# A ScalarE copy moved ahead of its slot's work, and the products of sixteen tokens moved to slots of their own, in a hybrid decoder layer with product-key experts

## The chip, the cores and the metric

The kernel runs on one core of one Trainium2 chip. A core has five engines that run their own instruction streams: TensorE (PE, with its weight loads as PEld), VectorE (DVE), ScalarE (ACT), GpSimd (POOL) and SyncE (SP), which here only issues DMAs. They meet through semaphores. The metric is the device time of one execution in microseconds; the median of three runs before the change is 1067.83 us (1067.64 to 1069.07).

## The reference

One decoder layer on 256 tokens of width 1024: attention of two kinds, gated and projected, then an expert layer. The change lies in the expert layer, of which this is the core:

```python
def peer_ffn(h, wq, subkeys, u, v):
    q = (hf @ wq).reshape(T, PEER_HEADS, 2, PEER_QDIM // 2)
    s = jnp.einsum('thpd,hpnd->thpn', q, subkeys).astype(jnp.float32)
    s1, i1 = lax.top_k(s[:, :, 0], PEER_TOPK)
    s2, i2 = lax.top_k(s[:, :, 1], PEER_TOPK)
    ...
    top_s, pos = lax.top_k(cand, PEER_TOPK)
    idx = jnp.take_along_axis(cand_idx, pos, axis=-1)
    w = jax.nn.softmax(top_s, axis=-1)
    ...
        act = jax.nn.gelu(jnp.einsum('cd,chkd->chk', x_c, u[idx_c]).astype(jnp.float32), approximate=False)
        coef = (w_c * act).astype(v.dtype)
        return jnp.einsum('chk,chkd->cd', coef, v[idx_c])
```

Each token chooses 16 of 128 x 128 experts in each of 8 heads, 128 choices in all. An expert is one row of u and one of v. Its number is a pair of keys below 128.

## The kernel before

**The dense form.** The kernel doesn't gather the experts' rows for most tokens. It multiplies all 16384 rows of u with the tokens, puts gelu on the result, multiplies it with each token's weight for that expert (zero for most), and then multiplies by all of v. Both matrices are read once, as 128 blocks of 128 experts. G[0] and G[1] hold the coefficients of blocks 0 to 63 and 64 to 127, each as 128 partitions x 64 blocks x 256 tokens in f32. The first 16 tokens (NG) go another way: their rows of u are gathered by indirect DMA, eight tokens at a time, the dot products are formed on VectorE, and their coefficients come to the blocks at the end. The other 240 tokens (TD) go through u in the dense form.

**Slots.** A slot (`slot`, L235) handles one block of weights. It issues the fetches of the blocks two and three ahead on SP's queue (L237, L238), then what is in `first`, then for the block two ahead the high part on ScalarE (L192, `whi`) and the low part on VectorE (L196, `wlo`), then what is in `late` (L250), then what is in `pre` (L251 to L253), and then the block's matmuls (L364: 24 of them, high part with the high and the low part of the tokens, low part with the high part). `raw`, `whi` and `wlo` have three buffers each. Each engine runs its instructions in the order in which they are issued here; only semaphores hold one back for another. So the order in a slot is written out by hand, and the place in the slot decides behind what an instruction stands on its engine.

**Two slots make a pair of u.** `u_pair` (L1211) puts the products of two blocks into one buffer `pj`, and one slot later, through `late`, `evac` brings them out with gelu: for the tokens whose weights are already in G to `gt` (L1227), then VectorE multiplies that into G (L1231); for the others to G itself (L1229). The first 32 pairs run while VectorE still chooses the experts. The change lies in the last 32 pairs, slots 0 to 63 of the second half of u. What runs in which of these slots is written out by `at_slot` (L1336 to L1355); jobs of one slot run in the order in which they were listed.

**The weights of the tokens come to the blocks as one-hot products.** For a group k of eight tokens (30 groups) VectorE makes one-hot rows of the first and the second keys (`hot_keys`, L1274) and multiplies the second with the weights, in f16 (`hot_high`, L1285). ScalarE makes the rest of the weight, four tokens in one slot and four in the next (`hot_low`, L1281). In slot 2k + 2 PE sums the 16 products (`hot_sum`, L1293) to a tile `pw` of two PSUM banks, of which there are two (`wide`, L1264). In slot 2k + 3 `hot_use` brings them to G: for the blocks whose gelu is there, VectorE multiplies into G (L1302, once for G[0] and once for G[1]); for the blocks that are still to come, ScalarE copies the product to G[1] (L1304), where gelu is multiplied on later. The one-hot tile has two buffers.

**The sixteen tokens.** `dot` (L1089) runs in every fourth slot, from 9 to 37, and asks for the next gather. `dots_end` and `coefs_in` bring the coefficients around through DRAM and one small transpose (L1118) in slots 39 and 42. Then, for each eight tokens, `few_keys` (L1312 twice, L1316 three times, VectorE), `few_sum` (L1322: 24 matmuls to a `pw` tile) and `few_use` (L1328, two copies on ScalarE to G[0] and G[1]). Their tables lie where the residual x2 lay; it was written to DRAM and comes back by four DMAs on POOL's queue (`x2_in`, L1073), which must wait for the last `few_sum`. The v stage after the last slot begins with transposes of x2 (L1406).

Of the kernel before, what the change touches and what calls it, by code (L numbers as in the profile page):

```python
# [14 lines left out]
AF = mybir.ActivationFunctionType  # L15
# [4 lines left out]
P = 128  # L20
# [10 lines left out]
TG = 8  # L31
PACE = 1.22
WARM = 15
WSCALE = 32768.0
# [103 lines left out]
def body(tc, nc, a):  # L138
# [137 lines left out]
    def table(f):  # L276
        nc.scalar.activation(junk, ones, f)
# [31 lines left out]
    def w1_load(j, hf):  # L309
        r = slice(8 * hf, 8 * hf + 8)  # L310
        nc.sync.dma_start(w1[:, j, r], a["w1"][:, j, r])
# [153 lines left out]
    def rope(name, dst, parts):  # L465
        raw = ropes[name]
        rp = bank("pS")
        nc.tensor.matmul(rp, K["rt"], flat(raw), start=True, stop=True)
        t = wk.tile([P, 2, T], F32, name="ropetmp", bufs=1)
        nc.vector.tensor_tensor(t, halves(rp), stab[:, None, :].to_broadcast([P, 2, T]), OP.mult)  # L470
        nc.vector.tensor_tensor(raw, raw, ctab[:, None, :].to_broadcast([P, 2, T]), OP.mult)
        dst = raw if dst is None else dst
        nc.vector.tensor_tensor(dst, raw, t, OP.add)
        halve(*parts, dst)
# [9 lines left out]
    def cmp_windows(j):  # L484
        win = wins[j] = wk.tile([P, 2, 8, 2, NCMP], F32, name="win")
        src = kcb[:, j].rearrange("p g (n l r) -> p g n l r", l=8, r=2)
        for hf in range(2):
            for g in range(2):
                nc.vector.tensor_tensor(
                    win[:, hf, :, g, :], src[:, g, hf:hf + NCMP, :, 0].rearrange("p n l -> p l n"),  # L490
                    pos[:, j, hf * 8:hf * 8 + 8, None].to_broadcast([P, 8, NCMP]), OP.add)

    def cmp_hidden(j):
        hp = bank("pS")
        for lp in range(16):
            nc.tensor.matmul(hp[:30, :P], flat(wins[j][:, lp // 8, lp % 8]), w1[:, j, lp], start=(lp == 0),  # L496
                             stop=(lp == 15))
        ht[j] = wk.tile([P, 30], F32, name="ht")
        hn = wk.tile([30, P], F32, name="hn")
        nc.scalar.activation(hn, hp[:30, :P], AF.Gelu)  # L500
        if j:
            table(AF.Exp)

        def back():
            tp = bank("pO")
            nc.tensor.transpose(tp[:, :30], hn, ident[:30, :30])
            nc.vector.tensor_copy(ht[j], tp[:, :30])
        backs.append(back)
# [208 lines left out]
    def y_turn(n, q2):  # L717
        tp = bank("pT")
        for j in range(2):
            cc = q2 * 2 + j  # L720
            for b in range(2):
                nc.tensor.transpose(tp[:, j * T + b * P:j * T + (b + 1) * P], y[:, b, n, cc * P:(cc + 1) * P], ident)
        c0 = n * 4 + q2 * 2
        hv = flat(bh[:, c0:c0 + 2])
        nc.scalar.activation(hv, tp, AF.Copy)
        nc.vector.tensor_tensor(flat(bl[:, c0:c0 + 2]), tp, hv.bitcast(F32), OP.subtract)
# [59 lines left out]
    def sv_evac(acc):  # L786
# [11 lines left out]
         pre=((fg_log, lambda: cmp_windows(0)), (lambda: table(AF.Gelu), fg_rest, lambda: rope("k", None, (krope[:, 0, 0], krope[:, 1, 0])), swap, lambda: cmp_windows(1), lambda: w1_load(1, 0))))  # L798
    pair(lambda pj: rope_in("q1", pj, 0.125), ah, al,
         pre=((lambda: cmp_hidden(0), fg_logs, lambda: w1_load(1, 1)), (cmp_back, lambda: cmp_hidden(1), lambda: rope("q0", nqt[:, 0:2], (nqs[:, 0, 0:2], nqs[:, 1, 0:2])))))  # L800
# [8 lines left out]
    for m in range(8):  # L809
        pre = [[tick], [tick]]  # L810
        if m == 5:
            pre = [[tick, lambda: y_turn(1, 0)], [tick, lambda: y_turn(1, 1)]]
        if m == 7:
            pre = [[], [lambda: y_turn(0, 0), lambda: y_turn(0, 1)]]
# [70 lines left out]
    G = [ga.tile([P, 64, T], F32, name="G0"), None]  # L885
# [173 lines left out]
    def tokens_out(q):  # L1059
        nc.gpsimd.dma_start(xhs[q].rearrange("(g t) d -> g t d", t=TG),  # L1060
                            xhd[None, q * TG:(q + 1) * TG, :].to_broadcast([P // TG, TG, D]))
# [5 lines left out]
    def x2_out(k):  # L1067
        sb, dr = x2_part(k)
        nc.gpsimd.dma_start(dr, sb)
# [5 lines left out]
    def tokens_in(q):  # L1075
        nc.gpsimd.dma_start(flat(x2[1]), xhs[q])
# [4 lines left out]
    def rows_in(n):  # L1081
        q, j = divmod(n, TG)
        nc.gpsimd.indirect_dma_start(rows_of_step(n), None, a["u_n"],
                                     bass.IndirectOffsetOnAxis(ap=sidx[:, q, j:j + 1], axis=0))
# [80 lines left out]
    def score(m):  # L1165
        pss = bank("pS")
        for b in range(2):
            tb = slice(b * P, (b + 1) * P)
            for j in range(2):
                nc.tensor.matmul(pss[:, (b * 2 + j) * P:(b * 2 + j + 1) * P], qs[m][:, j, tb],  # L1170
                                 subs[m][:, j * P:(j + 1) * P], start=True, stop=True)

        def out():
            for b in range(2):
                nc.scalar.activation(sc[:, b, 2 * m:2 * m + 2, :], pss[:, b * 256:b * 256 + 256].rearrange(
                    "p (j n) -> p j n", j=2), AF.Copy, scale=rn2[0][:, b:b + 1])
        late.append(out)
# [12 lines left out]
    for m in range(8):  # L1190
        first, second = [], []
# [16 lines left out]
    spots = {"blocks": 0, "tokens": 0}  # L1208
# [31 lines left out]
    for e in range(32):  # L1240
        pre = ((rows_out,), (io_tables,)) if e == 0 else ((lambda: score(7),), ()) if e == 1 else ((), ())
        if 4 <= e < 4 + 2 * NQ and e % 2 == 0:
            pre = (lambda: tokens_out((e - 4) // 2),), ()
        if 8 <= e < 16 and e % 2 == 0:
            pre = (lambda: x2_out((e - 8) // 2),), ()
        if e == 17:
            pre = (lambda: tokens_in(0),), ()
        if 22 <= e < 26:
            pre = (lambda: rows_in(e - 22),), ()
# [12 lines left out]
    hot = {}  # L1262
# [6 lines left out]
    spans = lambda k: slice(NG + k * TG, NG + (k + 1) * TG)  # L1269
# [18 lines left out]
    def hot_sum(k):  # L1288
# [4 lines left out]
                nc.tensor.matmul(pw[:, t * P:(t + 1) * P], E[:, 0, t], E[:, 2 - s, t], start=(s == 0), stop=(s == 1))  # L1293
        hot[k] = pw

    def hot_use(k):
        pv = hot.pop(k).rearrange("p (t i) -> p i t", t=TG)
        n = spots["blocks"]
        for i0, i1 in ((0, 64), (64, n)):
            if i1 > i0:  # L1300
                gv = G[i0 // 64][:, 0:i1 - i0, spans(k)]
                nc.vector.scalar_tensor_tensor(gv, pv[:, i0:i1], 1.0 / WSCALE, gv, OP.mult, OP.mult)  # L1302
        if n < P:
            nc.scalar.activation(G[1][:, n - 64:, spans(k)], pv[:, n:], AF.Copy, scale=1.0 / WSCALE)  # L1304
        spots["tokens"] += TG


# [25 lines left out]
    def at_slot(n, place, f, *v):  # L1333
        jobs.setdefault((n, place), []).append(lambda: f(*v))

    for k in range(ND):  # L1336
        at_slot(2 * k + 2, "pre", hot_sum, k)
        at_slot(2 * k + 3, "pre", hot_use, k)
        n = max(2 * k - 2, k)
        at_slot(n, "pre", hot_keys, k)  # L1340
        at_slot(n, "pre", hot_high, k)
        at_slot(2 * k - 1 if k else 0, "pre", hot_low, k, range(0, 4))
        at_slot(2 * k if k else 1, "pre", hot_low, k, range(4, 8))
# [3 lines left out]
    n = 9 + 4 * (TG - 1)  # L1347
    at_slot(n + 2, "pre", dots_end)
    at_slot(n + 5, "pre", coefs_in)
    for q in range(NQ):  # L1350
        at_slot(n + 7 + 3 * q, "pre", few_keys, q)
        at_slot(n + 9 + 3 * q, "pre", few_sum, q)
        at_slot(n + 10 + 3 * q, "pre", few_use, q)
    for k in range(4):
        at_slot(n + 14 + 2 * k, "pre", x2_in, k)  # L1355
    for e in range(32, 64):
        n = 2 * (e - 32)
        u_pair(e, *([jobs.pop((n + h, w), ()) for h in range(2)] for w in ("first", "pre")))
# [5 lines left out]
    pv = top.enter_context(tc.tile_pool(name="pv", bufs=4, space=PSUM, reuse_waits="tile"))  # L1364
# [44 lines left out]
    for k in range(P):  # L1409
        first = []  # L1410
# [73 lines left out]
```

## Time and profile before

| | us |
|---|---|
| median of the three runs | 1067.83 |
| the profiled execution | 1067.32 |
| its span, first to last instruction | 1065.5 |
| PE busy over the span | 1023.4 |
| PE's weight loads busy | 934.4 |
| DVE busy | 760.7 |
| ACT busy | 593.4 |
| last 32 pairs of u, 462.0 to 706.7 of the span: length | 244.7 |
| PE's weight loads busy in it | 203.43 |

The times inside the profile count from the start of the span. A busy engine is one that has an instruction running; matmuls are pipelined, so the busy time of the weight loads says more of how full TensorE is than that of the matmuls. A row of the timeline has the start, the duration, the engine, the line, the operation, out <- in with the shapes, how many were merged, and in brackets the idle time of the engine just before and what ended it. Over the whole span the chain of work that ended last is 70% PE, 16% DVE and 9% ACT.

### The profile page before, as it was taken

What the parts mean: (1) busy time and instruction counts of PE and PEld (TensorE: products, weight loads), DVE (VectorE), ACT (ScalarE), POOL (GpSimd) and SP (SyncE); (2) the same over time, 40 slices, a digit from 0 to 9 for tenths busy, and PEclk for the clock granted to TensorE, in tenths of its full rate; (3) what the DMA queues carried; (4) which work ended last, traced back from release to release, by engine and by line L of the source; (5) the groups of instructions that cost most, each with busy time, mean ns of one, the idle gap of its engine ahead of it and who ended that gap; (6) DMA issues with size and microseconds to landing.
All of it is one profiled execution on the core that took longest, in us unless ns stands there. A gap on an engine that the chain in (4) does not pass through costs nothing.

```text
span 1065.5 us, 18940 instructions
## 1 busy us (share of the span) xinstructions
PE 1023.4 (96%) x7394; PEld 934.4 (88%) x7394; DVE 760.7 (71%) x1423; ACT 593.4 (56%) x1090; POOL 50.6 (5%) x69
## 2 busy tenths in 40 slices
PE   9999999999999999999988868999999999999997
PEld 7898999999999999998878868988888888888885
DVE  5888677877989888867777777666665666656664
ACT  7545445565554747566666656554455544555444
POOL 3001010000100020300000100000000000000000
PEclk9999999999999999999999989999999999999999
DMA  8633435665576575854545434355555555555562
GB/s 278 218 101 102 132 111 155 190 189 182 192 255 213 190 262 184 287 179 149 177 155 174 146 113 159 131 170 194 197 197 188 190 195 198 192 192 191 195 217 99
DMA packets 54938, 192.87 MB, mean 181 GB/s; under 512 B 6512, under 2 KB 7968, under 8 KB 54816
## 3 DMA queue, kind: packets, MB, share of 16 engines
q1 hardware_dynamic: 48816, 175.27, 49.4%
q0 software_dynamic: 4448, 14.74, 4.5%
q10 hardware_dynamic: 1584, 1.64, 0.5%
q8 instruction: 58, 0.95, 0.4%
q14 instruction: 32, 0.26, 0.1%
HBM read 188.40 MB, written 3.23 MB: 180 GB/s over the span
## 4 chain that ended last, share of the span: by engine, by line
PE 70%; DVE 16%; ACT 9%; issue 3%; DMA 2%; DVEq 0%; SPq 0%; ACTq 0%
PE acc L1384 33%; PE pj L364 30%; DVE wlo L196 7%; ACT whi L192 4%; ACT onehot L1281 3%; DVE onehot L1274 3%; DVE G L1302 2%; DMA raw<-in_u_t 1%; PE pS L655 1%; DVE G L1231 1%; PE pT L627 1%; PE pS L496 1%; PE pS L1170 1%; DMA raw<-in_w_t 1%; DMA xg<-in_x 1%
## 5 line engine op out<-in xcount | busy, mean ns | idle before, releaser
L196 DVE TENSOR_TENSOR wlo<-raw,whi 128x1024 fp32r<-128x1024 f32 (+2 forms) x329 | 398.7, 1212 | 175.4 <-ACT whi L192 174.8
L192 ACT ACTIVATE whi<-raw 128x1024 fp32r<-128x1024 f32 (+2 forms) x329 | 342.7, 1043 | 105.1 <-PE pj L364 34.8
L364 PE MATMUL pj<-ah,whi 128*128 128x240 f32 (+1 forms) x1344 | 324.2, 283 | 0.4 <-ACT whi L192 0.2
L364 PE MATMUL pj<-al,whi 128*128 128x240 f32 (+1 forms) x1344 | 317.9, 279 | 0.1
L364 PEld LDWEIGHTS pj<-ah,whi 128*128 128x128 f32 x1344 | 256.1, 191 | 5.1 <-issue 1.2
L364 PEld LDWEIGHTS pj<-al,whi 128*128 128x128 f32 x1344 | 256.8, 191 | 1.8 <-issue 1.0
L364 PE MATMUL pj<-ah,wlo 128*128 128x240 f32 (+1 forms) x1344 | 181.5, 277 | 0.0
L364 PEld LDWEIGHTS pj<-ah,wlo 128*128 128x128 f32 x1344 | 166.5, 190 | 0.0
L1384 PE MATMUL acc<-whi,cl 128*128 128x512 f32 x512 | 158.5, 390 | 0.0
L1384 PE MATMUL acc<-whi,ch 128*128 128x512 f32 x512 | 158.5, 389 | 0.0
L1384 PE MATMUL acc<-wlo,ch 128*128 128x512 f32 x512 | 158.4, 389 | 0.0
L1372 ACT ACTIVATE ch<-G 128x256 fp32r<-128x256 f32 x128 | 53.4, 418 | 171.3 <-PE acc L1384 171.3
L1384 PEld LDWEIGHTS acc<-whi,cl 128*128 128x128 f32 x512 | 96.0, 188 | 20.4 <-DVE cl L1373 0.6
L1384 PEld LDWEIGHTS acc<-whi,ch 128*128 128x128 f32 x512 | 96.0, 188 | 20.2 <-ACT ch L1372 0.3
L1384 PEld LDWEIGHTS acc<-wlo,ch 128*128 128x128 f32 x512 | 96.1, 188 | 20.0
L1373 DVE TENSOR_TENSOR cl<-G,ch 128x256 fp32r<-128x256 f32 x128 | 54.4, 426 | 69.6 <-ACT ch L1372 69.6
L1281 ACT ACTIVATE onehot<-onehot,wl 128x128 f16<-128x128 f16 x240 | 76.2, 393 | 5.1 <-DVE onehot L1285 5.1
L1293 PE MATMUL pw<-onehot 128*128 128x128 f16 x480 | 47.6, 219 | 22.8 <-ACT onehot L1281 19.9
L1304 ACT ACTIVATE G<-pw 128x496 f32<-128x496 f32 (+29 forms) x30 | 11.7, 391 | 88.1 <-DVE G L1302 88.1
L1293 PEld LDWEIGHTS <-onehot 128*128 128x128 f16 x480 | 30.0, 97 | 32.4 <-issue 24.0
L364 PE MATMUL pj<-bh,whi 128*128 128x256 f32 x192 | 48.0, 286 | 0.0
L364 PE MATMUL pj<-bl,whi 128*128 128x256 f32 x192 | 47.4, 284 | 0.0
(316 smaller groups left out, 919.7 us busy)
## 6 DMA issues: line engine op xcount, KB each, us to landing
raw<-in_u_t SPq DMA_DIRECT2D x128, 512.0 KB, 3.3
raw<-in_v_n SPq DMA_DIRECT2D x128, 512.0 KB, 3.2
raw<-in_w_m SPq DMA_DIRECT2D x16, 512.0 KB, 3.6
raw<-in_w_q SPq DMA_DIRECT2D x16, 512.0 KB, 3.7
raw<-in_w_t SPq DMA_DIRECT2D x15, 512.0 KB, 4.5
raw<-in_w_b SPq DMA_DIRECT2D x8, 512.0 KB, 3.5
raw<-in_w_o SPq DMA_DIRECT2D x8, 512.0 KB, 3.6
sg<-in_w SPq DMA_DIRECT2D x4, 512.0 KB, 6.3
```

The source lines that it names most:

```text
L192: return [lambda s=slice(u, min(v, n)): nc.scalar.activation(hi[:, s], raws[k][:, s], AF.Copy) for u, v in cuts]
L196: nc.vector.tensor_tensor(lo[:, cs], raws[k][:, cs], hi[:, cs].bitcast(F32), OP.subtract)
L364: nc.tensor.matmul(out, (wl if v == 2 else wh)[:, c], (l if v == 1 else h)[:, c], start=(i == 0), stop=(i == len(seq) - 1))
L496: nc.tensor.matmul(hp[:30, :P], flat(wins[j][:, lp // 8, lp % 8]), w1[:, j, lp], start=(lp == 0), stop=(lp == 15))
L1274: nc.vector.tensor_tensor(pairs(E[:, 0:2].rearrange("p s t i -> p (s t) i")), numbers(2 * TG), v[:, :, None, :].to_broadcast([P, 2 * TG, 6 ...
L1281: nc.scalar.activation(E[:, 1, t], E[:, 1, t], AF.Copy, scale=wl[:, n:n + 1])
L1293: nc.tensor.matmul(pw[:, t * P:(t + 1) * P], E[:, 0, t], E[:, 2 - s, t], start=(s == 0), stop=(s == 1))
L1302: nc.vector.scalar_tensor_tensor(gv, pv[:, i0:i1], 1.0 / WSCALE, gv, OP.mult, OP.mult)
L1304: nc.scalar.activation(G[1][:, n - 64:, spans(k)], pv[:, n:], AF.Copy, scale=1.0 / WSCALE)
L1372: nc.scalar.activation(ch, g, AF.Copy)
L1373: nc.vector.tensor_tensor(cl, g, ch.bitcast(F32), OP.subtract)
L1384: nc.tensor.matmul(acc[2 * b + d], (cl if q == 1 else ch)[:, tb], (vl if q == 2 else vh)[:, cs], start=False, stop=last and q == 2, skip_g ...
```

## The change

`hot_use` loses its ScalarE copy. A new job `hot_copy` issues the same copy, over the same blocks and tokens, in `first` of the same slot 2k + 3: ahead of the high part of the block two ahead, where it stood behind the low part and VectorE's products. The number of blocks that are done is the same at both places, since `evac` runs in the even slots.

The jobs of the sixteen tokens move. With n = 37 the keys go from slots 44 and 47 to 45 and 49, the sums from 46 and 49 to 47 and 51, the copies to G from 47 and 50 to 48 and 52. The sums of the other tokens are in even slots, so the first of the two sums (46) shared its slot with one of them and now has an odd slot. The four loads of x2 go from slots 51, 53, 55, 57 to 53, 55, 57, 59.

```diff
+    def hot_copy(k):
+        pv = hot[k].rearrange("p (t i) -> p i t", t=TG)
+        n = spots["blocks"]
+        if n < P:
+            nc.scalar.activation(G[1][:, n - 64:, spans(k)], pv[:, n:], AF.Copy, scale=1.0 / WSCALE)
+
     def hot_use(k):
         pv = hot.pop(k).rearrange("p (t i) -> p i t", t=TG)
         n = spots["blocks"]
@@
                 gv = G[i0 // 64][:, 0:i1 - i0, spans(k)]
                 nc.vector.scalar_tensor_tensor(gv, pv[:, i0:i1], 1.0 / WSCALE, gv, OP.mult, OP.mult)
-        if n < P:
-            nc.scalar.activation(G[1][:, n - 64:, spans(k)], pv[:, n:], AF.Copy, scale=1.0 / WSCALE)
         spots["tokens"] += TG
@@
         at_slot(2 * k + 2, "pre", hot_sum, k)
+        at_slot(2 * k + 3, "first", hot_copy, k)
         at_slot(2 * k + 3, "pre", hot_use, k)
@@
     for q in range(NQ):
-        at_slot(n + 7 + 3 * q, "pre", few_keys, q)
-        at_slot(n + 9 + 3 * q, "pre", few_sum, q)
-        at_slot(n + 10 + 3 * q, "pre", few_use, q)
+        at_slot(n + 8 + 4 * q, "pre", few_keys, q)
+        at_slot(n + 10 + 4 * q, "pre", few_sum, q)
+        at_slot(n + 11 + 4 * q, "pre", few_use, q)
     for k in range(4):
-        at_slot(n + 14 + 2 * k, "pre", x2_in, k)
+        at_slot(n + 16 + 2 * k, "pre", x2_in, k)
```

## The prediction

> **What bounds the kernel now.** The view by stages comes first. Its columns are the stretch, the busy time of PE, PE's weight loads, DVE, ACT and POOL, then the granted PE clock, the DMA share and GB/s.
>
> ```profile
> core 0: us, PE busy (x) PEld busy (x) DVE busy (x) ACT busy (x) POOL busy (x), PEclk, DMA share, GB/s
> 284.00:455.00 171.00, 170.77 (x1523) 170.58 (x1522) 149.81 (x444) 95.28 (x119) 21.07 (x22) 1.00 0.69 235
> 467.00:480.00 13.00, 13.00 (x136) 12.93 (x135) 7.45 (x12) 8.53 (x22) 0.00 (x0) 1.00 0.42 148
> 552.00:568.00 16.00, 14.03 (x130) 13.00 (x130) 11.86 (x17) 10.41 (x27) 0.94 (x1) 1.00 0.53 165
> 612.00:620.00 8.00, 6.89 (x51) 6.21 (x50) 5.49 (x7) 5.06 (x13) 0.00 (x0) 0.81 0.38 129
> 710.00:1060.00 350.00, 348.23 (x1534) 287.59 (x1534) 211.47 (x266) 176.76 (x264) 1.34 (x1) 1.00 0.56 188
> ```
>
> Before 455 and after 710 PE is full. Between them, in the second half of u, which the change touches, the weight loads fill 13.00 of 16.00 us (552 to 568), and no other engine is full: some loop of waits sets the pace. The chain of waits from 540 to 600, and the group of the copy that the change moves, show which.
>
> ```profile
> by line: DVE wlo L196 28.6%; DVE onehot L1274 15.3%; ACT onehot L1281 14.9%; issue 13.5%; ACT whi L192 12.9%; DVE G L1302 10.7%; DVE G L1231 3.9%; DVE onehot L1285 0.7%; ACT G L1304 0.6%; DVEq L196 0.5%; ACTq L1227 0.2%; ACTq L192 0.0%
> L1304 ACT ACTIVATE G<-pw 128x496 f32<-128x496 f32 (+29 forms) x30 | 11.7, 391 | 88.1 <-DVE G L1302 88.1
> ```
>
> PE has no share in the chain at all, and ACT stood still 88.1 us before the thirty copies, each time until VectorE's product (L1302) was done. One round (two slots: two blocks of u, one group of eight tokens) in the timeline, as start, duration, engine, line:
>
> ```profile
> 561.42 1.22 DVE L196 TENSOR_TENSOR wlo<-raw,whi 128x1024 fp32r<-128x1024 f32 x1
> 562.56 0.96 DVE L1302 SCALAR_TENSOR_TENSOR G<-pw,G 128x512 f32<-128x512 f32 x2
> 563.55 0.42 ACT L1304 ACTIVATE G<-pw 128x304 f32<-128x304 f32 x1 [2.81 <-DVE G L1302]
> 563.87 1.27 ACT L1281 ACTIVATE onehot<-onehot,wl 128x128 f16<-128x128 f16 x4
> 565.04 1.05 ACT L192 ACTIVATE whi<-raw 128x1024 fp32r<-128x1024 f32 x1
> 566.12 1.22 DVE L196 TENSOR_TENSOR wlo<-raw,whi 128x1024 fp32r<-128x1024 f32 x1 [2.60 <-ACT whi L192]
> 566.49 1.27 ACT L1281 ACTIVATE onehot<-onehot,wl 128x128 f16<-128x128 f16 x4
> 566.94 1.09 PE L1293 MATMUL pw<-onehot 128*128 128x128 f16 x7 [0.94 <-ACT onehot L1281]
> 567.26 0.37 DVE L1231 TENSOR_TENSOR G<-G,gt 128x208 f32<-128x208 f32 x1
> 567.55 1.22 DVE L1274 TENSOR_TENSOR onehot<-io,keys 128x2048 f16<-128x2048 f16 x1
> 567.66 1.05 ACT L192 ACTIVATE whi<-raw 128x1024 fp32r<-128x1024 f32 x1
> 568.80 0.69 DVE L1285 TENSOR_TENSOR onehot<-onehot,wt 128x1024 f16<-128x1024 f16 x1
> 569.41 1.22 DVE L196 TENSOR_TENSOR wlo<-raw,whi 128x1024 fp32r<-128x1024 f32 x1
> 571.56 0.41 ACT L1304 ACTIVATE G<-pw 128x288 f32<-128x288 f32 x1 [2.85 <-DVE G L1302]
> ```
>
> The loop closes: DVE's low part and product, 561.42 to 563.52 (2.10); ACT's copy, four one-hot rows and next high part until DVE may go on at 566.12 (2.60); DVE's low part, L1231, keys and one-hot, 566.12 to 569.41 (3.29). That is 7.99 us, the distance of the two low parts. DVE waits 2.60 for ACT and ACT 2.8 for DVE in each round; PE waits for the rows (L1281) that ACT does late.
>
> What PE needs by itself stands where the stage begins, with PE still ahead:
>
> ```profile
> 467.01 0.90 PEld L1293 LDWEIGHTS <-onehot 128*128 128x128 f16 x16
> 469.65 0.97 PEld L364 LDWEIGHTS pj<-ah,wlo 128*128 128x128 f32 x8
> 472.34 0.97 PEld L364 LDWEIGHTS pj<-ah,wlo 128*128 128x128 f32 x8
> 473.34 0.90 PEld L1293 LDWEIGHTS <-onehot 128*128 128x128 f16 x16
> ```
>
> One slot is 472.34 - 469.65 = 2.69, a round 473.34 - 467.01 = 6.33, so the one-hot sum costs 6.33 - 2 x 2.69 = 0.95.
>
> **The change part by part.** *The copy* keeps its thirty instructions (11.7 us of ACT) and goes ahead of the slot's high part (L192). SP's fetches are issued before it in the slot, as before; it passes no DMA. Its new wait is for PE's sum (L1293) of the slot before. Behind it on ACT stands the high part, which must wait for PE anyway: it writes the buffer that the slot before reads, and that slot's matmuls come behind the same sum. So this wait can hold up nothing that wasn't held already. I take 0; the other end is the 2.8 that it waits now, all gain lost. DVE's product now waits for the copy, but DVE's low part ahead of it needs the high part, which ACT issues behind the copy: hidden.
>
> What is late next? ACT's work per round is 563.55 to 567.66 plus 1.05, 5.16 us. DVE's is 2.10 + 3.29 = 5.39, and these rows add to it; the last line is the weights' DMA with its size and its time to landing:
>
> ```profile
> 571.45 1.21 DVE L1089 SCALAR_TENSOR_TENSOR x<-x,x 128x1024 f32<-128x1024 f32 x1
> 695.28 0.62 DVE L1231 TENSOR_TENSOR G<-G,gt 128x448 f32<-128x448 f32 x1
> 697.91 1.23 DVE L1302 SCALAR_TENSOR_TENSOR G<-pw,G 128x512 f32<-128x512 f32 x2
> raw<-in_u_t SPq DMA_DIRECT2D x128, 512.0 KB, 3.3
> ```
>
> At the end it is 5.39 + (0.62 - 0.37) + (1.23 - 0.96) = 5.91. In every second round of the first half a dot adds 1.21: 6.60, or 6.0 on the mean of two rounds. The loop that is left (one-hot, rows 1.17, high 1.05, low 1.14, L1231 0.29, keys 1.25, one-hot 0.69) is 5.6. All are under PE's 6.33, and a dot's excess of 0.27 is smaller than the slot by which high and low parts run ahead. So **PE becomes the bound, at 6.33 a round**. The weights' DMA then has to bring 512 KB per 3.17 us, 165 GB/s, where the stage before 455 moved 235, and it lands in 3.3 us, with three buffers to land in.
>
> *The sixteen tokens' products* move to slots 45, 47, 48 and 49, 51, 52 (from 44, 46, 47 and 47, 49, 50).
>
> ```profile
> 629.97 1.14 PEld L1293 LDWEIGHTS <-onehot 128*128 128x128 f16 x10
> 635.30 1.28 DVE L1312 TENSOR_TENSOR x<-io,keys 128x1024 bf16<-128x1024 f16 x2
> 636.62 2.02 DVE L1316 TENSOR_TENSOR x<-x,cs 128x1024 bf16<-128x1024 bf16 x3
> 638.56 1.22 DVE L196 TENSOR_TENSOR wlo<-raw,whi 128x1024 fp32r<-128x1024 f32 x1
> 641.20 0.37 PE L1322 MATMUL pw<-x,x 128*128 128x128 bf16 x2 [7.41 <-ACT G L1304]
> 649.44 0.10 PEld L1293 LDWEIGHTS <-onehot 128*128 128x128 f16 x1
> 653.45 1.34 PEld L1322 LDWEIGHTS <-x 128*128 128x128 bf16 x24
> 655.27 2.22 POOL L1073 DMA_DIRECT2D x<-x2s x4 [46.94 <-PE pw L1322]
> 658.96 1.05 PE L1293 MATMUL pw<-onehot 128*128 128x128 f16 x16 [1.24 <-ACT G L1304]
> 705.80 1.06 PE L364 MATMUL pj<-ah,wlo 128*128 128x240 f32 x8
> ```
>
> Now the first product (slot 46) shares its slot with a one-hot sum and waits 7.41 for one of the two pw buffers. Alone in slot 47 it finds its buffer free, but the sum of slot 48 then needs the one that DVE's product of slot 47 lets go. From the start of slot 44, PE reaches slot 48 after 6.33 + 0.95 + 2.69 + 1.34 + 2.69 = 14.0 us. DVE: high part behind PE's slot 44 at 3.64 + 1.0, low 1.14, product 1.1, the five key operations 3.26 (635.30 to 638.56) gives 10.2; low, L1231, keys, one-hot 3.5; low 1.14, product 1.1: 15.9. So PE waits some 2 us, and again in slot 52. The ends are 0 and 7.41 each; 1.24 (658.96, the same wait behind a product in its own slot) is nearest, I take 2.0. ACT's two copies of 1.1 lie in its spare time. POOL's four loads of x2 wait in fact for the second product; some 38 us stay until u ends, against 2.22 us of issue: hidden.
>
> The sum for the profiled execution (1067.32; span 1065.5 and 1.8 around it, untouched): from 467.01, 28 rounds x 6.33 = 177.2, last sum and four slots 0.95 + 4 x 2.69 = 11.7, two products 2 x 1.34 = 2.7, the small transpose 0.2, waits 4.0: u ends at 467.0 + 195.8 = 662.8, where it ended at 705.80 and eight loads later, 706.7. Gain 43.9, so 1023.4; the median of the runs shown (1067.83) lies 0.5 higher: **1024.0**. The v stage, full on PE, only comes earlier.
>
> On short gaps, the row 612 to 620 grants 0.81 though its PE waits are about 1.2 us. By that row each 2 us wait could cost another 8.0 x 0.19 = 1.5 us, 3 in all: 1027, inside the range. The Trainium skill ("TensorE: Matmul & The Clock Gate", "What's actually happening") halves the clock only after an idle window of about 3.4 us, by which the two waits cost nothing more: 1024; the row differs from it.
>
> **The rivals.**
>
> *DVE's wait takes the place of ACT's, and DVE becomes the bound.* The product and the copy write separate blocks, so the 88.1 us come from their common buffer pw, and order between the two stays. If DVE waits out the copy, its round is 5.39 + 0.39 = 5.8, and 7.0 with a dot. With 6.6 on 28 rounds that costs 7.6, with 7.0 it costs 19: 1031 to 1043, likeliest 1035. For it: DVE's margin is only 0.3 in dot rounds; against: the copy is issued a whole high part ahead of the product. The Trainium skill ("PSUM — Partial Sum Buffer", "PSUM bank collisions raise a hardware error") says that reads by two engines of one bank must be kept apart too; the thirty waits agree, and by it the wait turns round rather than goes.
>
> *The copy isn't freed*: it also shares G1 with DVE's L1231 and earlier products. If the loop stays at 8.0, only the products' slots count. Now 629.97 to 649.44 is 19.5 us for a round and a product, 8.0 + 1.3 without waits; of the 10 lost, 4 come back as waits: 1062 or so. Against it: L1231 ends before the keys, three operations before the loop would need it.
>
> *Slower: a lower clock.* PE's 196 us from slot 4 on become dense; at a clock c they take 196/c. The gain of 44 is gone at 196 x (1/c - 1) = 44, c = 0.817, and 0.79 gives 1076. For it: 0.81 was granted at 612 to 620. Against: 1.00 for 171 us and for 350 us of full PE.
>
> **How the numbers follow.** The forecast (1018 to 1034: waits from 0 to 7.4 each, a slow stretch or two) gets 0.78, the DVE bound 0.14, the unfreed copy 0.04, no change at all 0.02 (the loop is the chain, so hardly), the clock 0.02. The range 1018 to 1037 takes the forecast and half of the first rival, about 0.85. A measurement of this kernel can tell about 0.2% (2.1 us) from no change: faster 0.78 + 0.14 + 0.04 = 0.96, same 0.02, slower 0.02.
>
> **What would show it.** Right: hardly any idle time before the copy; sums (L1293) 6.33 apart; weight loads full from 467 to the end of u, near 663; PE in the chain there; waits of some 2 us before two sums behind the products. DVE bound: rounds of 6.6 to 7 with ACT and DVE in the chain. Unfreed: idle time before the copy stays near 88. Clock: under 0.9 over the stage. The forecast is wrong if PE's rounds stay over 6.6 at full clock, or if loads of weights land late.

## The result and the profile after

| | before | after |
|---|---|---|
| median, us | 1067.92 (1067.64 to 1069.07, 4 runs) | 1021.86 (1019.87 to 1022.48, 4 runs) |
| profiled execution, us | 1067.32 | 1019.87 |
| its span, us | 1065.5 | 1018.1 |
| last u matmul ends, us of the span | 706.7 | 660.3 |

The ratio is 0.9564, 95% interval 0.9547 to 0.958. The forecast was 1024.0 in a range of 1018 to 1037. The medians here and below are of all executions; ratios and intervals leave out two that lie far above the rest, 1139.13 us of the kernel before and 5292.97 us of the experiment products_only.

From the page of the kernel after, the busy times and the chain that ended last:

```profile
span 1018.1 us, 18964 instructions
PE 1003.4 (99%) x7394; PEld 926.0 (91%) x7394; DVE 761.1 (75%) x1423; ACT 597.3 (59%) x1090; POOL 53.8 (5%) x69
PE 93%; DVE 4%; ACT 2%; DMA 1%; issue 0%; DVEq 0%; ACTq 0%
L1281 ACT ACTIVATE onehot<-onehot,wl 128x128 f16<-128x128 f16 x240 | 76.4, 392 | 18.3 <-DVE onehot L1285 17.6
```

DVE and ACT do what they did before (760.7 and 593.4 us then), in a span 47 us shorter, and PE has gone from 70% to 93% of the chain. The stages, with the columns of the table in the prediction:

```profile
467.00:480.00 13.00, 13.00 (x133) 12.94 (x133) 11.41 (x18) 12.53 (x32) 0.00 (x0) 1.00 0.54 176
552.00:568.00 16.00, 16.00 (x167) 15.91 (x167) 14.87 (x21) 13.83 (x36) 1.68 (x1) 1.00 0.65 227
600.00:620.00 20.00, 18.53 (x203) 18.24 (x202) 19.22 (x26) 13.13 (x33) 0.37 (x1) 1.00 0.39 120
```

From 552 to 568 the weight loads fill 15.91 of 16.00 us where they filled 13.00. DVE is close behind (14.87), and from 600 to 620, where the sixteen tokens' keys are made, it is the fuller of the two. One round in the timeline after; the copy is L1300 now and VectorE's product L1308:

```profile
541.25 1.23 DVE L196 TENSOR_TENSOR wlo<-raw,whi 128x1024 fp32r<-128x1024 f32 x1 [0.61 <-ACT whi L192]
541.62 1.27 ACT L1281 ACTIVATE onehot<-onehot,wl 128x128 f16<-128x128 f16 x4
542.79 0.40 ACT L1300 ACTIVATE G<-pw 128x288 f32<-128x288 f32 x1
543.77 1.06 ACT L192 ACTIVATE whi<-raw 128x1024 fp32r<-128x1024 f32 x1 [0.57 <-PE pj L364]
544.74 1.26 ACT L1281 ACTIVATE onehot<-onehot,wl 128x128 f16<-128x128 f16 x4
544.86 1.22 DVE L196 TENSOR_TENSOR wlo<-raw,whi 128x1024 fp32r<-128x1024 f32 x1 [0.24 <-ACT whi L192]
546.00 0.98 DVE L1308 SCALAR_TENSOR_TENSOR G<-pw,G 128x512 f32<-128x512 f32 x2
```

The copy follows the rows without a gap. What ACT waits for in this round is PE (0.57 before the high part); over the whole span it also waits for DVE's one-hot, 17.6 us by the page's row above. DVE's product starts when its own low part is done, not when the copy is. All thirty copies together waited this long, by the view of the copy's line:

```profile
L1300 ACT ACTIVATE G<-pw x30: 197/378/567, 464.7 to 649.7; 128x496 f32<-128x496 f32 x1, 128x480 f32<-128x480 f32 x1, 128x464 f32<-128x464 f32 x1, 128x448 f32<-128x448 f32 x1
its engine sat idle before it (us, times) until:
  PE pw L1293: 0.2, 1
```

0.2 us, where it was 88.1. PE's sums, the second of the thirty, with which the stage is under way, two in the middle, the two behind the sixteen tokens' products, and the last:

```profile
464.52 0.89 PEld L1293 LDWEIGHTS <-onehot 128*128 128x128 f16 x16
540.81 0.90 PEld L1293 LDWEIGHTS <-onehot 128*128 128x128 f16 x16
547.15 0.90 PEld L1293 LDWEIGHTS <-onehot 128*128 128x128 f16 x16
607.79 0.90 PEld L1293 LDWEIGHTS <-onehot 128*128 128x128 f16 x16 [1.66 <-DVE G L1308]
623.13 0.89 PEld L1293 LDWEIGHTS <-onehot 128*128 128x128 f16 x16 [1.25 <-DVE G L1308]
648.54 0.90 PEld L1293 LDWEIGHTS <-onehot 128*128 128x128 f16 x16
```

A round is 547.15 - 540.81 = 6.34 us, and just two sums wait.

### The profile page after: what moved, and what is told of

It is laid out like the page before. It is cut to its first block, busy times and chain, and to the rows that moved or that the text cites. A ratio compares the mean times of both kernels' runs of the same rounds, so it can differ in the third digit from the quotient of the medians.

```text
span 1018.1 us, 18964 instructions
## 1 busy us (share of the span) xinstructions
PE 1003.4 (99%) x7394; PEld 926.0 (91%) x7394; DVE 761.1 (75%) x1423; ACT 597.3 (59%) x1090; POOL 53.8 (5%) x69
## 4 chain that ended last, share of the span: by engine, by line
PE 93%; DVE 4%; ACT 2%; DMA 1%; issue 0%; DVEq 0%; ACTq 0%
PE pj L364 47%; PE acc L1389 34%; PE pw L1293 3%; DVE wlo L196 1%; DMA raw<-in_u_t 1%; PE pS L655 1%; ACT whi L192 1%; PE pT L627 1%; PE pS L496 1%; PE pS L1170 1%; PE pO L286 1%; PE pO L638 0%; PE pO L639 0%; PE pj L760 0%; PE pj L757 0%
## 5 line engine op out<-in xcount | busy, mean ns | idle before, releaser
L1281 ACT ACTIVATE onehot<-onehot,wl 128x128 f16<-128x128 f16 x240 | 76.4, 392 | 18.3 <-DVE onehot L1285 17.6
L1293 PE MATMUL pw<-onehot 128*128 128x128 f16 x480 | 33.3, 220 | 4.1 <-DVE G L1308 2.5
L622 ACT ACTIVATE prob<-pS,nm 128x128 f32<-128x128 f32 (+1 forms) x48 | 19.7, 416 | 29.1 <-DVE nm L619 29.1
L1274 DVE TENSOR_TENSOR onehot<-io,keys 128x2048 f16<-128x2048 f16 x30 | 36.6, 1220 | 0.0
```

What stands on the lines that cost most here:

```text
L622: nc.scalar.activation(p[:, o], src[b], AF.Exp, bias=nm[:, b:b + 1], accum_out=sums[:, b, h:h + 1])
L1274: nc.vector.tensor_tensor(pairs(E[:, 0:2].rearrange("p s t i -> p (s t) i")), numbers(2 * TG), v[:, :, None, :].to_broadcast([P, 2 * TG, 6 ...
L1281: nc.scalar.activation(E[:, 1, t], E[:, 1, t], AF.Copy, scale=wl[:, n:n + 1])
```

## The experiments

Each time stands beside runs of the kernel before on the same chip (medians 1068.94 for the first four, 1068.87 for the others). The changed kernel's 1021.86 stands beside other runs of the kernel before (1067.92), so a difference of a few us from it is uncertain by about 1 us.

| | median, us | ratio to before, 95% interval |
|---|---|---|
| copy_only | 1024.58 | 0.9601 (0.9577 to 0.9624) |
| products_only | 1065.59 | 0.9967 (0.9953 to 0.9982) |
| copy_behind_high | 1021.39 | 0.9571 (0.9546 to 0.9596) |
| no_second_product | 1058.42 | 0.9919 (0.9892 to 0.9945) |
| vector_more_061 | 1037.55 | 0.9703 (0.9687 to 0.9718) |
| vector_more_125 | 1053.72 | 0.9858 (0.9843 to 0.9873) |
| products_other_banks | 1020.70 | 0.9546 (0.9528 to 0.9564) |
| groups_later | 1017.21 | 0.9521 (0.9506 to 0.9537) |

### Each half of the change alone

copy_only is the changed kernel with the sixteen tokens' jobs back at their old slots:

```diff
-        at_slot(n + 8 + 4 * q, "pre", few_keys, q)
-        at_slot(n + 10 + 4 * q, "pre", few_sum, q)
-        at_slot(n + 11 + 4 * q, "pre", few_use, q)
+        at_slot(n + 7 + 3 * q, "pre", few_keys, q)
+        at_slot(n + 9 + 3 * q, "pre", few_sum, q)
+        at_slot(n + 10 + 3 * q, "pre", few_use, q)
...
-        at_slot(n + 16 + 2 * k, "pre", x2_in, k)
+        at_slot(n + 14 + 2 * k, "pre", x2_in, k)
```

> The copy at its new place, the sixteen tokens' products at their old slots. Theory (the copy's place alone opens the loop between ScalarE and VectorE, TensorE becomes the bound): rounds of 6.34 us and no idle time before the copy; the first product again shares a slot with a one-hot sum and finds its buffer late, some 5 us of waits at the products where the changed kernel has 2.9, so 1022 to 1027 us. Rival (the products' new slots carry a good part of the gain): 1032 us or more.

It took 1024.58. Its first product and the sum behind the second, in the timeline of PE's weight loads (the product is L1326 here):

```profile
605.88 1.34 PEld L1326 LDWEIGHTS <-x 128*128 128x128 bf16 x24 [2.88 <-DVE G L1308]
621.60 0.90 PEld L1293 LDWEIGHTS <-onehot 128*128 128x128 f16 x16 [1.22 <-DVE G L1308]
```

So there are 2.88 + 1.22 = 4.1 us of waits where the changed kernel has 2.9. The old slots cost a wait of about 1 us more, not the 7.41 that stood there before: that wait ended with ACT's copy, by its row in the prediction, and the copy no longer waits for DVE. The medians lie 2.7 us apart, of which these rows show 1.2. In the profiled execution of copy_only PE was also granted only 0.71 of its clock from 460 to 464 and 0.87 from 464 to 468, where the changed kernel's had 1.00 in both: 4 x 0.29 + 4 x 0.13 = 1.7 us. Whether the medians hold this too isn't shown.

products_only is the kernel before with the reverse of that diff, the copy at its old place.

> The products of the sixteen tokens at their new slots, the copy at its old place. Theory: the loop stays at 8.0 us a round and the 88 us of idle time before the copy stay; only the waits around the first product go, 1060 to 1066 us. Rival (the products' slots carry a good part): 1055 us or less.

It took 1065.59, about 3 us less than before. From its list of waits:

```profile
ACT G L1304 <- DVE G L1302: 86.2, 30, 4.2
```

The wait of the copy is whole (86.2 us in thirty waits). The products' slots alone give 0.3%; the copy's place gives nearly all.

### What made the copy wait, and what place it needs

copy_behind_high moves the copy behind the slot's high part, yet ahead of VectorE's product:

```diff
-        at_slot(2 * k + 3, "first", hot_copy, k)
+        at_slot(2 * k + 3, "pre", hot_copy, k)
```

> The changed kernel with the copy behind the slot's high part but still issued ahead of VectorE's product. Theory (what counts is which of the two reads pw first; the copy ends while VectorE is at its low part): no idle time before the copy but that for TensorE, rounds of 6.34 us, 1020 to 1025 us. Rival (the place ahead of the high part is what counts: the copy then lands behind a wait for TensorE and VectorE's product waits for it): 1030 us or more, with VectorE idle before its product.

1021.39, the same as the change. Its timeline, ACT and DVE in an odd slot:

```profile
545.15 1.06 ACT L192 ACTIVATE whi<-raw 128x1024 fp32r<-128x1024 f32 x1 [0.88 <-PE pj L364]
546.12 0.39 ACT L1300 ACTIVATE G<-pw 128x288 f32<-128x288 f32 x1
546.25 1.23 DVE L196 TENSOR_TENSOR wlo<-raw,whi 128x1024 fp32r<-128x1024 f32 x1 [0.25 <-ACT whi L192]
547.39 0.98 DVE L1308 SCALAR_TENSOR_TENSOR G<-pw,G 128x512 f32<-128x512 f32 x2
```

The copy ends at 546.5, in the shadow of DVE's low part, and the product waits for nothing. So "first in its slot" isn't what counts; it is enough that the copy is issued before the product.

no_second_product is the kernel before with VectorE writing only G[0], so that the copy shares nothing but pw with the product ahead of it:

```diff
-        for i0, i1 in ((0, 64), (64, n)):
+        for i0, i1 in ((0, 64),):
```

> The kernel before, with VectorE's second product of each group (into G[1]) left out, so that the copy and VectorE's product share only the buffer pw and no longer the tile G[1]. Theory (the wait comes from the common pw): the copy still waits some 80 us in all for VectorE, the round is shorter by the product that is left out (0.28 us on the mean, 8 us in all), 1055 to 1063 us. Rival (the wait comes from the common tile G[1]): no wait, TensorE bound, 1020 to 1030 us.

1058.42, and in its list of waits:

```profile
ACT G L1304 <- DVE G L1302: 78.4, 30, 5.9
```

All thirty waits remain, though the two write to different tiles. The common buffer pw is enough to order the two readers, and in the kernels before and after the one that is issued first goes first; in the kernel after, DVE never stands idle before the product, so the order costs nothing there. The Trainium skill ("PSUM — Partial Sum Buffer", "PSUM bank collisions raise a hardware error") says that two engines' reads of a bank must be kept apart; these thirty waits agree. A kernel in which only G[1] is shared wasn't tried.

### How far PE is ahead of the next bound

vector_more_061 does VectorE's one-hot multiplication of each group twice, vector_more_125 the comparison of the keys; the second only repeats the first:

```diff
+        for again in range(2):
-        nc.vector.tensor_tensor(pairs(E[:, 2]), pairs(E[:, 1]),
-                                wt[:, spans(k), None, :].to_broadcast([P, TG, 64, 2]), OP.mult)
+            nc.vector.tensor_tensor(pairs(E[:, 2]), pairs(E[:, 1]),
+                                    wt[:, spans(k), None, :].to_broadcast([P, TG, 64, 2]), OP.mult)
```

> The changed kernel with VectorE's one-hot multiplication done twice in each group (the second does the same again, 0.61 us from start to start). VectorE is busy 181 us in the 202 us of this stage; thirty more of these make 199. Theory (TensorE is the bound with VectorE close behind, 0.3 us a round where the dots are): the rounds with dots and the late ones grow over TensorE's 6.34 us, 3 to 10 us more, 1025 to 1032 us, with VectorE coming into the chain. Rival (a wide margin): under 1024 us, TensorE alone in the chain.

> The changed kernel with VectorE's comparison of the keys done twice in each group (1.25 us from start to start, 37 us in all). VectorE then needs 218 us in a stage of 202. Theory: VectorE is the bound, 16 us and its waits more, 1038 to 1050 us, rounds of about 6.6 to 8.1 us. Rival (a wide margin, or waits that hide it): under 1030 us.

Both came out above what was expected: 1037.55 (15.7 more than the change) and 1053.72 (31.9 more). From the timeline of vector_more_061, a round without a dot:

```profile
546.70 1.22 DVE L1274 TENSOR_TENSOR onehot<-io,keys 128x2048 f16<-128x2048 f16 x1
547.95 1.42 DVE L1286 TENSOR_TENSOR onehot<-onehot,wt 128x1024 f16<-128x1024 f16 x2
549.29 1.22 DVE L196 TENSOR_TENSOR wlo<-raw,whi 128x1024 fp32r<-128x1024 f32 x1
549.46 1.28 ACT L1281 ACTIVATE onehot<-onehot,wl 128x128 f16<-128x128 f16 x4 [1.97 <-DVE onehot L1286]
550.65 1.05 ACT L192 ACTIVATE whi<-raw 128x1024 fp32r<-128x1024 f32 x1
551.73 1.23 DVE L196 TENSOR_TENSOR wlo<-raw,whi 128x1024 fp32r<-128x1024 f32 x1 [0.34 <-ACT whi L192]
```

Two multiplications take 549.29 - 547.95 = 1.34, so the second costs 0.73, not 0.61: each takes 0.69, and by these rows the second starts only when the first, whose output it writes again, has ended. Thirty cost 21.9 us, of which 15.7 reached the end: 6.2 us were hidden. In the other run 30 x 1.25 = 37.5 were added and 31.9 arrived: 5.6 hidden. Two doses give about the same answer: some 6 us of added work on DVE are hidden in the whole stage. They are not spread evenly over the rounds. Two stretches of vector_more_061 and one line of its list of waits (the product is L1327 here, its tables L1321):

```profile
552.00:568.00 16.00, 15.68 (x152) 14.57 (x150) 15.56 (x21) 12.62 (x33) 1.68 (x1) 1.00 0.56 196
600.00:620.00 20.00, 14.77 (x144) 13.99 (x143) 19.40 (x32) 13.71 (x35) 0.00 (x0) 0.91 0.41 132
PEld L1327 <- DVE x L1321: 4.6, 1, 4.6
```

From 552 to 568, where DVE has dots, the weight loads fill 14.57 us (15.91 in the changed kernel) and DVE is busy 15.56 of 16.00: its own work is the bound there. The loop that the prediction put at 5.6 us shows too: with 0.73 more it is as long as PE's round, and in the rows above ACT waits 1.97 for DVE's one-hot and DVE 0.34 for ACT's high part. From 600 to 620, where the sixteen tokens' keys are made, the weight loads fill 13.99 us (18.24 in the changed kernel): DVE is full, PE waits 4.6 us for its tables, and the granted clock is 0.91. The sums on both sides of the two products lie 15.98 and 10.45 us apart, 9.45 and 9.00 in the changed kernel, so half of the 15.7 us arrives in these two rounds. The rounds at the start of the stage (seven, 6.33 to 6.51 us) and at its end (four, 6.33 to 6.40) hide nearly all of theirs.

### Versions that go on from the change

products_other_banks puts the sixteen tokens' products into the two banks of the small transposes:

```diff
-        pw = wide()
+        two = hot["few", q] = [bank("pO"), bank("pO")]
...
-                nc.tensor.matmul(pw[:, t * P:(t + 1) * P], few[0][:, 0, t], v, start=(k == 0), stop=(k == 2))
-        hot["few", q] = pw
+                nc.tensor.matmul(two[t // 4][:, t % 4 * P:(t % 4 + 1) * P], few[0][:, 0, t], v, start=(k == 0), stop=(k == 2))
...
+        for j, half in enumerate(hot.pop(("few", q))):
+            pv = half.rearrange("p (t i) -> p i t", t=4)
+            for k in range(2):
+                nc.scalar.activation(G[k][:, :, q * TG + 4 * j:q * TG + 4 * j + 4], pv[:, 64 * k:64 * k + 64], AF.Copy)
```

> The changed kernel with the sixteen tokens' products in the two banks that the small transposes use (pO), so that they take no pw buffer. Theory (the waits of 1.66 and 1.25 us before two sums come from the two pw buffers): both waits go, 1018 to 1020 us. Rival (they come from VectorE being 3.3 us late with the keys, whatever the buffer): 1021 to 1023 us with the waits elsewhere.

1020.70, with an interval that overlaps the change's: not told apart. The waits before the sums are gone; in their place stand shorter ones of the second product for its tables, in PE's timeline:

```profile
619.22 0.22 PE L1326 MATMUL pO<-x,x 128*128 128x128 bf16 x1 [0.27 <-DVE x L1320]
619.94 0.22 PE L1326 MATMUL pO<-x 128*128 128x128 bf16 x1 [0.51 <-DVE x L1320]
```

The 2.9 us became 0.8 (1.0 by the weight loads), and DVE's late keys are the rest: theory and rival were each right in part.

groups_later keeps that and puts the groups' sums, copies and products one round later, and their keys too, except those of the first group, which stay in slot 0:

```diff
-        at_slot(2 * k + 2, "pre", hot_sum, k)
-        at_slot(2 * k + 3, "first", hot_copy, k)
-        at_slot(2 * k + 3, "pre", hot_use, k)
-        n = max(2 * k - 2, k)
-        at_slot(n, "pre", hot_keys, k)
-        at_slot(n, "pre", hot_high, k)
-        at_slot(2 * k - 1 if k else 0, "pre", hot_low, k, range(0, 4))
-        at_slot(2 * k if k else 1, "pre", hot_low, k, range(4, 8))
+        at_slot(2 * k + 4, "pre", hot_sum, k)
+        at_slot(2 * k + 5, "first", hot_copy, k)
+        at_slot(2 * k + 5, "pre", hot_use, k)
+        at_slot(2 * k, "pre", hot_keys, k)
+        at_slot(2 * k, "pre", hot_high, k)
+        at_slot(2 * k + 1, "pre", hot_low, k, range(0, 4))
+        at_slot(2 * k + 2, "pre", hot_low, k, range(4, 8))
```

> As products_other_banks, and the thirty groups one round later: keys in slot 2k, rows in 2k + 1 and 2k + 2, sum in 2k + 4, copy and product in 2k + 5. Theory (the 2 to 4 us that TensorE loses around 455 to 464, waiting for the first rows and at a lower clock, come from the first groups' short lead): 2 to 3 us less than products_other_banks, 1015 to 1018 us. Rival (the end pays it back, since VectorE's last product then lies in the last slot before the v stage): 1018 to 1021 us with TensorE waiting at the start of v.

1017.21, ratio 0.9521 with an interval clear of the change's: it beats both kernels. Its interval and that of products_other_banks, which took 3.5 us more, overlap a little (0.9537 and 0.9528). The stages at the start, of groups_later:

```profile
456.00:460.00 4.00, 4.00 (x38) 3.98 (x36) 1.29 (x2) 2.41 (x7) 0.00 (x0) 1.00 0.87 336
460.00:464.00 4.00, 4.00 (x46) 3.99 (x44) 2.90 (x3) 3.42 (x9) 0.00 (x0) 1.00 0.48 146
```

and of the changed kernel:

```profile
456.00:460.00 4.00, 2.92 (x24) 2.06 (x24) 2.21 (x2) 2.92 (x8) 0.00 (x0) 1.00 0.71 274
460.00:464.00 4.00, 4.00 (x38) 4.00 (x37) 1.67 (x3) 3.09 (x8) 0.00 (x0) 1.00 0.37 131
```

and of products_other_banks:

```profile
456.00:460.00 4.00, 2.61 (x21) 1.45 (x20) 1.71 (x3) 3.39 (x9) 0.00 (x0) 1.00 0.86 333
460.00:464.00 4.00, 4.00 (x23) 4.00 (x23) 1.82 (x2) 2.11 (x5) 0.00 (x0) 0.61 0.49 159
```

The weight loads fill 3.98 of 4.00 us from 456 to 460, where the first groups' wait left 2.06 and 1.45. From 460 to 464 products_other_banks was granted 0.61 of the clock besides, so part of the 3.5 us lies in the clock; how much of it in the medians isn't shown. The rival's price at the start of v did not come: the 16 transposes of x2 there run without a wait:

```profile
654.92 1.91 PE L1410 MATMUL acc<-ident,x 128*128 128x128 f32 x16
```

## Why the prediction was right

**What bounded the kernel.** Right, and shown from both sides: with the copy issued first the 88.1 us of waits are 0.2 and the round goes from 8.0 to 6.34; with the products' slots alone they stay and the time hardly moves.

**The copy's new wait at 0.** Right: 0.2 us in all, and nothing behind it was held (copy_behind_high differs by less than the spread).

**PE the bound at 6.33 a round.** Right: 6.34, and the chain from 470 to 655 in the kernel after says so by lines:

```profile
by line: PE pj L364 83.2%; PE pw L1293 13.9%; PE pw L1326 1.5%; DVE G L1308 1.2%; DVE wlo L196 0.2%; PE pO L1118 0.1%; issue 0.0%; DVEq L196 0.0%
```

**The sum.** From the second sum to the last the forecast has 177.2 + 2.7 + 0.2 + 4.0 = 184.1 us; measured were 648.54 - 464.52 = 184.0. Two small misses cancel: the waits behind the products were 1.66 + 1.25 = 2.9, not 4.0, and the 28 rounds without them took 184.0 - 2.9 - 2.9 = 178.2, 6.36 each, not 6.33. The stage ends at 660.3, not 662.8, because it also began 2.5 us earlier (464.52, not 467.01), ahead of the first moved copy. That stretch the prediction left as it was, and the last section says what differs there. The profiled execution ended 3.5 us below its forecast of 1023.4: 2.5 from this start, and 1.0 behind u, which takes 358.8 us to the end before and 357.8 after. The prediction had the v stage only come earlier. In the kernel before PE also waited there for the gelu of the last pair, by its list of waits:

```profile
PEld acc L1406 <- ACT gt L1227: 0.8, 1, 0.8
```

The kernel after has no such wait. The median lies nearer to its forecast, 2.1 us below, only because it is 2.0 above the profiled execution where the forecast added 0.5; that is luck.

**The rivals.** DVE's wait didn't take the place of ACT's, since DVE's low part still stands ahead of the product; in copy_behind_high it alone covers the copy. But the rival's ground, DVE's margin, was thin as it said: 6 us in the stage. The expectation of vector_more_061 was too low because it set DVE's busy time against the whole stage (199 in 202 us), while DVE was already full where the sixteen tokens' keys are made (19.22 of 20.00 us from 600 to 620), and half of what arrived did so there. The clock stayed at 1.00 in the stages above.

## What to carry to other kernels

Where two engines read one PSUM buffer, look whether the order in which their instructions are issued is an order in time, as it was here; issue first the one that is ready first, and look whether the other has work ahead of it that covers the turn. A loop of waits shows as no engine full and a chain without the busiest engine in it; what opening it is worth is the distance to the next bound's pace, which a stretch where the bound runs undisturbed gives directly (6.33 us here). Then add a known cost to the runner-up to see how near the next bound is: here some 6 us in the stage, so a slower VectorE soon costs, and a faster one is worth at most the waits for it that are left (2.9 us). An average over a stage doesn't say where the cost will arrive.

## What the runs showed that was not expected

The waits of the first groups are much alike in the kernels before and after, and the clock behind them is not. The stretch 460 to 464 of the kernel before:

```profile
460.00:464.00 4.00, 4.00 (x23) 4.00 (x23) 1.76 (x2) 2.17 (x6) 0.00 (x0) 0.57 0.39 135
```

PE got 0.57 of its clock there, and 23 weight loads; the kernel after got 1.00 and 37 in its row above, behind much the same waits, none of them over 1.1 us:

```profile
459.02 0.74 PEld L1293 LDWEIGHTS <-onehot 128*128 128x128 f16 x6 [1.09 <-issue]
```

That is the longest of them in the kernel before; in the kernel after it is 1.09 too. Fourteen loads of 0.11 us are 1.5 us, so that part of the 2.5 us that the stage began earlier is luck of the clock in one execution. Most of the rest stood there before: the first group's keys (L1274) start at 454.47 in the kernel before and at 453.56 in the kernel after. Of the ten profiled executions five were granted 0.50 to 0.74 of the clock from 460 to 464, the other five 1.00, groups_later, which has no such waits, among these. The Trainium skill ("TensorE: Matmul & The Clock Gate", "What's actually happening") has the clock judged in windows that run free of the kernel, which would fit two outcomes behind the same waits. It has the clock halved after an idle window of about 3.4 us; here it fell to 0.57 with no wait over 1.1 us, and where the two differ the measurement decides.
